# The first eight row tiles of the input projection multiplied before their normalisation is known

## The chip, the cores and the metric

One core of one Trainium2 chip. The time is the device time of one execution in microseconds (us), three executions of the kernel before: 811.78, 812.30 and 813.51 us, median 812.3 us. The profile is of a fourth execution.

## The reference, cut to what matters

One layer: modulated RMSNorm, one input projection, two groups of heads, one output projection, residual, a last RMSNorm. Only the first two matter here, and of the projection only the columns of the convolution group.

```
mod_lat = silu(c) @ w_ada + b_ada             # 2048 x 6144
sh_l, sc_l, gt_l = split(mod_lat, 3)
hl = rmsnorm(x, norm_g) * (1 + sc_l) + sh_l    # x: 512 tokens x 2048
bl, cl, ul, gl, vl, ql = split(hl @ w_in)      # 2048 x 6144
ya = bl * conv(cl * ul) * silu(gl)
```

Everything is float32. With r the reciprocal root of a token's mean square and g = norm_g * (1 + sc), a column of the product is the sum over the 2048 rows k of w[k] * (x[k] * g[k] * r + sh[k]). The factor r belongs to the token and is the same for every k; the shift belongs to k and is the same for every token.

## The kernel before, in words

All activations lie transposed: 128 features on the partitions, 512 tokens along the free axis, so the 2048 rows of the projection are 16 row tiles, k = 0 to 15. A float32 product is taken as three matmuls of rounded parts (`mm3`, lines 81 to 85): weights and activations are split into a high and a low part, and high*high, low*high and high*low are added up in one accumulator (PSUM).

Stage A (lines 343 to 365) runs row tile by row tile over seven column tiles (`A_TILES`), with seven accumulators `acc[0]` to `acc[6]` open over all 16 rows. Before row k can be multiplied, TensorE computes its modulation from 2 MB of `w_ada`: `ada(k)` (line 216) is 64 small float32 matmuls into the accumulator tile `aux`, 128 records in the trace. VectorE turns them round (`ada_t`, line 226: `mods`, `gs`, `sh`); VectorE and ScalarE form the normalised row `x*gs*rinvB + sh` and split it (`h_lat`, line 271: tiles `xhi`, `hlo`). The weights of the row (`raw`, 448 KB) are split by ScalarE and VectorE (`split_a`: `whi`, `wlo`). In each turn k the order on TensorE is: column tile 0 of row k, `ada(k+1)`, column tiles 1 to 6 of row k.

Ahead of stage A stands the statistic: all 16 blocks of x are loaded first (line 98, 256 KB each), squared in turn by VectorE and ScalarE (lines 240 and 242) and summed by TensorE (line 246); four columns of mean squares go through `rsqrt_cols` (line 174) and are spread by TensorE to `rinvB`, 128 x 512 (lines 250 to 262). `ada(0)` and the first row follow.

All loads are issued by SP in program order. The modulation weights `rada` have six buffers of 1 MB (three rows), so the load of row k+3 waits until `ada(k)` has read its own; `raw` has five buffers.

After stage A, stage BC (line 616 on) multiplies the other column tiles piece by piece with the same 16 split rows, which therefore stay in memory; the seven accumulators of stage A are read in its first turns by the functions `ev_c`, `ev_u`, `ev_b`, `ev_g` (lines 388 to 413). Context rows are loaded in turns 12 and 13 of stage A, squared by ScalarE (`ctx_sq`), added by GpSimd (line 295), and summed by TensorE (line 300) in stage BC's turn 2.

Of the kernel before, what the change touches and what calls it, by code (L numbers as in the profile page):

```python
# [16 lines left out]
T = 512  # L17
# [26 lines left out]
N_D = 32  # L44
N_GT = 32
NHC = 3


@with_exitstack
def tile_hybrid_layer(ctx, tc, xt, ct, xn, wada, wgt, bgt, wa_, wbc, wout, lruw, par, ident, fg, out):  # L50
# [10 lines left out]
    hc = s_ctx.enter_context(p_ctx)  # L61
    ctx.enter_context(tc.manual_schedule())
# [31 lines left out]

    xl, xc = [], []
    for k in range(KT):
        t = hl.tile([128, T], F32, name="xhi", bufs=17)
        nc.sync.dma_start(t, xt[k])
        if k == 5:
            nc.sync.dma_start(pt, par)  # L100
            nc.sync.dma_start(idt, ident)
        xl.append(t)
    rawa, rawq = {}, {}
# [84 lines left out]
    gq = [None]  # L188

    def split_a(k):  # L190
        wsp["a", k] = split(rawq.pop(("a", k)), NA * 128)

    def first_operands():

        n, raw, x = NA * 128, rawq.pop(("a", 0)), xl[0]
        whi = stage.tile([128, 1024], F32R, name="whi", bufs=3)
        wlo = stage.tile([128, 1024], F32R, name="wlo", bufs=3)
        hi = hl.tile([128, T], F32R, name="xhi", bufs=17)
        lo = hl.tile([128, T], F32R, name="hlo")
        nc.scalar.copy(whi[:, :n], raw[:, :n])  # L200
        nc.vector.scalar_tensor_tensor(x, x, gs[:, 0, 0:1], rinvB, op0=ALU.mult, op1=ALU.mult)
        nc.scalar.activation(hi, x, AF.Identity, bias=sh[:, 0, 0:1])  # L202
        nc.vector.tensor_tensor(wlo[:, :n], raw[:, :n], whi[:, :n].bitcast(F32), op=ALU.subtract)
        nc.vector.scalar_tensor_tensor(lo, x, sh[:, 0, 0:1], hi.bitcast(F32), op0=ALU.add, op1=ALU.subtract)
        wsp["a", 0], hlat[0] = (whi, wlo), (hi, lo)

    for g in range(3):
        for p in range(2):
            load_ada(g, p)
        load_wa(g)  # L210

# [3 lines left out]

    def ada(g):

        o = aux[:, 64 * (g % 2):64 * (g % 2) + 64]
        for p in range(2):
# [16 lines left out]

    for k in range(KT):
        sq = ta.tile([128, T], F32, name="sq", bufs=3)
        if k % 2:
            nc.vector.tensor_tensor(sq, xl[k], xl[k], op=ALU.mult)  # L240
        else:
            nc.scalar.activation(sq, xl[k], AF.Square)
        if k == 8:
            silu_c()
        j = k % 4
        nc.tensor.matmul(acc[6][32 * j:32 * j + 32, :], ones32, sq, start=k < 4, stop=k >= KT - 4,
                         skip_group_check=True)
    warm(3)
    ssum = ta.tile([128, T], F32, name="sq", bufs=3)
    nc.vector.tensor_copy(ssum, acc[6])  # L250
    for j in range(4):
        nc.tensor.matmul(acc[5][:, 2 * j:2 * j + 2], ssum[:, 128 * j:128 * j + 128], cmean[:, 0:2],
                         start=True, stop=True, skip_group_check=True)
    ms = ta.tile([128, 4], F32, name="ms")
    nc.vector.tensor_scalar(ms, acc[5][:, 0:8:2], EPS, None, op0=ALU.add)
    rl = rsqrt_cols(ta, ms, 4, "l")
    ada(0)
    ada_t(0)
    for j in range(4):
        nc.tensor.transpose(acc[4][:, 128 * j:128 * j + 128], rl[:, j:j + 1].to_broadcast([128, 128]), idt)  # L260
    rinvB = ta.tile([128, T], F32, name="rinvB", bufs=1)
    nc.scalar.copy(rinvB, acc[4])
    warm(8)

    def make_h(k, v, x, rb, n, hi, lo):
        nc.vector.scalar_tensor_tensor(x, x, gs[:, k, v:v + 1], rb, op0=ALU.mult, op1=ALU.mult)  # L266
        nc.scalar.activation(hi, x, AF.Identity, bias=sh[:, k, v:v + 1])  # L267
        nc.vector.scalar_tensor_tensor(lo, x, sh[:, k, v:v + 1], hi.bitcast(F32), op0=ALU.add,
                                       op1=ALU.subtract)

    def h_lat(k):
        hi = hl.tile([128, T], F32R, name="xhi", bufs=17)
        lo = hl.tile([128, T], F32R, name="hlo")
        make_h(k, 0, xl[k], rinvB, T, hi, lo)
        hlat[k] = (hi, lo)
# [138 lines left out]

# [416 lines left out]
```

## Time and profile before

| | |
|---|---|
| median of three runs | 812.3 us |
| profiled execution, its own time | 810.92 us |
| its span | 809.1 us |
| TensorE matmuls busy | 786.8 us (97%), 5712 records |
| VectorE busy | 480.4 us (59%) |
| ScalarE busy | 366.8 us (45%) |
| GpSimd busy | 89.7 us (11%) |

The span is cut into 40 equal slices of 20.2 us in the page; in the first five the 16 DMA engines are busy nine tenths or more of the time, and TensorE is at 7 to 9 tenths. From stage BC on TensorE is at 9 tenths in every slice but the last. The profiled execution's time is 1.8 us more than its span, which begins and ends with the first and last instruction.

### The profile page before, as it was taken

The page shows a single profiled execution, that of the slowest core. Times are in us where ns is not written, and L with a number is a line of the kernel's source. Part 1 is how long each engine was busy: PE and PEld are TensorE (multiplying, and loading weights), DVE is VectorE, ACT ScalarE, POOL GpSimd, SP SyncE. Part 2 cuts the span into 40 slices and gives each one's busy share as a digit, 9 for nine tenths or more (in the row PEclk, how much of TensorE's full clock was granted, in tenths as well). Part 3 has the DMA queues.
Part 4 walks back from the last instruction along what each step waited for, and adds up shares of the span by engine and source line. Part 5 has one row for each costly group of instructions (what it writes and reads, how often), then busy time and mean ns, then how long its engine had stood idle before and what let it go on. Part 6 is the DMA issues. An engine that isn't in the chain of part 4 may idle for free.

```text
span 809.1 us, 13525 instructions
## 1 busy us (share of the span) xinstructions
PE 786.8 (97%) x5712; PEld 678.2 (84%) x5712; DVE 480.4 (59%) x643; ACT 366.8 (45%) x458; POOL 89.7 (11%) x64
## 2 busy tenths in 40 slices
PE   7899899999999999999999999999999999999995
PEld 2688687889999998888888888888888888888884
DVE  3644444888688677283829474666476834253665
ACT  4312224451111125768576857575858532222234
POOL 0000002500000000212020202020212002020200
PEclk9999999999999999999999999999999999999999
DMA  9999996225655664232323232323231753323205
GB/s 352 417 417 415 347 353 218 98 79 187 227 184 180 226 222 153 79 116 80 120 76 122 96 121 79 118 78 118 79 124 58 309 185 92 116 81 128 79 0 208
DMA packets 36494, 136.31 MB, mean 168 GB/s; under 512 B 4049, under 2 KB 6353, under 8 KB 31697
## 3 DMA queue, kind: packets, MB, share of 16 engines
q1 hardware_dynamic: 36434, 135.45, 47.0%
q8 instruction: 45, 0.74, 0.4%
q14 instruction: 15, 0.12, 0.0%
HBM read 131.24 MB, written 4.19 MB: 167 GB/s over the span
## 4 chain that ended last, share of the span: by engine, by line
PE 95%; DMA 1%; DVE 1%; issue 1%; ACT 1%; SPq 0%; ACTq 0%
PE bacc L83 22%; PE bacc L84 22%; PE bacc L85 21%; PE bacc L741 6%; PE bacc L742 6%; PE bacc L743 6%; PE bacc L223 4%; DMA xhi<-in_xt 1%; PE plru L470 1%; PE plru L468 1%; PE plru L85 1%; PE plru L742 1%; PE plru L741 1%; PE plru L84 1%; PE plru L83 1%; PE plru L743 1%
## 5 line engine op out<-in xcount | busy, mean ns | idle before, releaser
L84 PE MATMUL bacc<-xhi,wlo 128*128 128x512 f32 x736 | 280.5, 381 | 2.4 <-issue 1.8
L83 PE MATMUL bacc<-xhi,whi 128*128 128x512 f32 x736 | 281.0, 382 | 0.8 <-ACT xhi L202 0.4
L85 PE MATMUL bacc<-hlo,whi 128*128 128x512 f32 x736 | 279.2, 379 | 2.6 <-issue 2.5
L74 DVE TENSOR_TENSOR wlo<-raw,whi 128x1024 fp32r<-128x1024 f32 (+1 forms) x129 | 157.6, 1225 | 198.9 <-ACT whi L73 197.6
L73 ACT CAST whi<-raw 128x1024 fp32r<-128x1024 f32 (+1 forms) x129 | 132.7, 1031 | 211.6 <-PE bacc L85 116.3
L84 PEld LDWEIGHTS bacc<-xhi,wlo 128*128 128x128 f32 x736 | 139.1, 189 | 25.2 <-DVE wlo L74 5.1
L85 PEld LDWEIGHTS bacc<-hlo,whi 128*128 128x128 f32 x736 | 139.1, 189 | 22.7 <-issue 2.9
L83 PEld LDWEIGHTS bacc<-xhi,whi 128*128 128x128 f32 x736 | 139.1, 189 | 22.5 <-ACT whi L73 0.7
L741 PE MATMUL bacc<-whi,yhi 128*128 128x512 f32 x224 | 85.1, 380 | 0.5 <-DVE dg L671 0.5
L742 PE MATMUL bacc<-wlo,yhi 128*128 128x512 f32 x224 | 84.9, 379 | 0.0
L743 PE MATMUL bacc<-whi,ylo 128*128 128x512 f32 x224 | 84.9, 379 | 0.0
L478 POOL TENSOR_TENSOR li<-li,xb 128x768 f32<-128x768 f32 x16 | 30.8, 1925 | 365.3 <-ACT li L475 365.3
L474 ACT ACTIVATE lr<-plru,pt 64x768 f32<-64x768 f32 x32 | 28.7, 895 | 53.2 <-PE plru L471 53.0
L267 ACT ACTIVATE xhi<-xhi,sh 128x512 fp32r<-128x512 f32 x15 | 10.8, 723 | 85.9 <-DVE xhi L266 85.9
L741 PEld LDWEIGHTS bacc<-whi,yhi 128*128 128x128 f32 x224 | 42.3, 189 | 7.1 <-DVE dg L671 1.1
L743 PEld LDWEIGHTS bacc<-whi,ylo 128*128 128x128 f32 x224 | 42.3, 189 | 6.0
L742 PEld LDWEIGHTS bacc<-wlo,yhi 128*128 128x128 f32 x224 | 42.3, 189 | 6.0
L518 DVE SCALAR_TENSOR_TENSOR gacc<-raw,cs,gacc 128x1024 f32<-128x1024 f32 x32 | 39.6, 1278 | 0.0
L223 PEld LDWEIGHTS bacc<-rada,cs 128*32 128x32 f32 x2048 | 29.6, 110 | 6.8 <-issue 6.8
L84 PE MATMUL bacc<-xchi,wlo 128*128 128x256 f32 x128 | 35.2, 275 | 0.0
L85 PE MATMUL bacc<-hclo,whi 128*128 128x256 f32 x128 | 35.2, 275 | 0.0
L83 PE MATMUL bacc<-xchi,whi 128*128 128x256 f32 x128 | 35.2, 275 | 0.0
(168 smaller groups left out, 876.3 us busy)
## 6 DMA issues: line engine op xcount, KB each, us to landing
raw<-in_wbc SPq DMA_DIRECT2D x82, 512.0 KB, 3.5
rada<-in_wada SPq DMA_DIRECT2D x32, 1024.0 KB, 10.4
raw<-in_wgt SPq DMA_DIRECT2D x32, 512.0 KB, 4.7
raw<-in_wout SPq DMA_DIRECT2D x32, 512.0 KB, 3.5
raw<-in_wa_ SPq DMA_DIRECT2D x16, 448.0 KB, 11.2
xhi<-in_xt SPq DMA_DIRECT2D x16, 256.0 KB, 4.5
xr<-in_xn SPq DMA_DIRECT2D x4, 1024.0 KB, 7.7
xchi<-in_ct SPq DMA_DIRECT2D x16, 128.0 KB, 4.4
```

Source lines behind the costliest of these rows:

```text
L73: nc.scalar.copy(hi[:, :n], raw[:, :n])
L74: nc.vector.tensor_tensor(lo[:, :n], raw[:, :n], hi[:, :n].bitcast(F32), op=ALU.subtract)
L83: nc.tensor.matmul(acc, wh, hh, start=first, stop=False)
L84: nc.tensor.matmul(acc, wl, hh, start=False, stop=False)
L85: nc.tensor.matmul(acc, wh, hl, start=False, stop=last)
L223: nc.tensor.matmul(o[32 * q:32 * q + 32], cs[:, 8 * p + j, :], r[:, j, q, :], start=p + j == 0, stop=p + j == 8, skip_group_check=True)
L474: nc.scalar.activation(lru["r", d][o], pf[0:64, :TA], AF.Sigmoid, bias=b[0:64])
L478: nc.gpsimd.tensor_tensor(lru["i", d], lru["i", d], xb[m], op=ALU.mult)
L518: nc.vector.scalar_tensor_tensor(gacc[:, s], gtq.pop(i), cs[:, k, 0:1], gacc[:, s], op0=ALU.mult, op1=ALU.add)
L741: nc.tensor.matmul(accs[t], yh[:, ts], wh, start=kk == 0, stop=False)
L742: nc.tensor.matmul(accs[t], yh[:, ts], wl, start=False, stop=False)
L743: nc.tensor.matmul(accs[t], yl[:, ts], wh, start=False, stop=kk == KT - 1)
```

## The change

Rows 0 to 7 are multiplied without r and without shift: `h_early` forms and splits `x*gs` alone. When row 7 is done, each of the seven accumulators is multiplied in place by `rinvB` (`scale_acc`). The share of the shift of these rows, the sum over k of sh[k]*w[k], is gathered by VectorE over the raw weights (`z_acc`, tile `zt`, 128 x 896), summed over the partitions by seven matmuls (`z_sum`) into `bz`, and comes in as a bias when the accumulators are read (`ev_c`, `times`). Rows 8 to 15 are made as before. Since stage BC needs all 16 rows normalised, `h_lat(k-8)` makes the early rows again in turns 8 to 15.

The statistic is moved into the rows: x is loaded in groups of three with the rows (`X_ROWS`), squared by ScalarE alone and added by GpSimd (`x_sq`); in turn 6 two matmuls with a matrix of ones (`lat_stat`) give the sum on all partitions, and `lat_rsqrt` takes the root and the reciprocal on 128 x 512 elements. The order of a turn on TensorE becomes: column tiles 0 to 2, `ada(k+1)`, column tiles 3 to 6. `split_a(k+1)` is moved to the start of the turn, ahead of `ada_t(k+1)`.

```diff
+EARLY = 8
+X_ROWS = [0, 3, 3, 3, 3, 3]
...
+    def load_row(r):
+        for _ in range(X_ROWS[r] if r < len(X_ROWS) else 0):
+            load_x()
+        load_ada(r, 0)
+        load_wa(r)
+        load_ada(r, 1)
...
+    def x_sq(k):
+        if k == 0:
+            nc.scalar.activation(sqa, xl[k], AF.Square)
+            return
+        t = te.tile([128, T], F32, name="sq", bufs=3)
+        nc.scalar.activation(t, xl[k], AF.Square)
+        nc.gpsimd.tensor_tensor(sqa, sqa, t, op=ALU.add)
+    def lat_stat(a, b):
...
+        nc.tensor.matmul(aux[:, :b - a], onesr.bitcast(F32), sqa[:, a:b], start=True, stop=True,
+                         skip_group_check=True)
+        nc.vector.tensor_scalar(st["ms"][:, a:b], aux[:, :b - a], 1.0 / D, EPS, op0=ALU.mult, op1=ALU.add)
+    def lat_rsqrt():
...
+        nc.scalar.activation(u, ms, AF.Sqrt)
+        nc.vector.reciprocal(rinvB, u)
+        nc.vector.tensor_tensor(u, rinvB, rinvB, op=ALU.mult)
+        nc.vector.tensor_tensor(u, u, ms, op=ALU.mult)
+        nc.vector.tensor_scalar(u, u, -0.5, 1.5, op0=ALU.mult, op1=ALU.add)
+        nc.vector.tensor_tensor(rinvB, rinvB, u, op=ALU.mult)
+    def scale_acc(j):
+        a = acc[j].rearrange("p (b a) -> p b a", a=2)
+        nc.vector.tensor_tensor(a, a, pairs(rinvB), op=ALU.mult)
+    def z_acc(k):
...
+            nc.vector.scalar_tensor_tensor(zt, raw, sh[:, k, 0:1], zt, op0=ALU.mult, op1=ALU.add)
+    def z_sum():
+        for j in range(NA):
+            nc.tensor.matmul(aux[:, 2 * j:2 * j + 2], zt[:, 128 * j:128 * j + 128], onesr.bitcast(F32)[:, 0:2],
+                             start=True, stop=True, skip_group_check=True)
+        nc.vector.tensor_copy(bz[:, :NA], aux[:, 0:2 * NA:2])
+    def h_early(k):
...
+        nc.scalar.activation(hi, x, AF.Copy, scale=g)
+        nc.vector.scalar_tensor_tensor(lo, x, g, hi.bitcast(F32), op0=ALU.mult, op1=ALU.subtract)
...
+    split_a(0)
+    ada(0, (0,))
+    warm(20)
+    ada(0, (1,))
     ada_t(0)
+    h_row(0)
+    warm(14)
...
     for k in range(KT):
+        if k + 1 < KT:
+            split_a(k + 1)
+        else:
+            split_piece(0)
+        if k == EARLY:
+            z_sum()
+        while n_sq < min(KT, 1 + sum(X_ROWS[:k + 1])):
+            x_sq(n_sq)
+            n_sq += 1
+        if k >= EARLY:
+            h_lat(k - EARLY)
         main_a(k, 0)
+        if k == EARLY - 2:
+            lat_stat(0, 384)
+        main_a(k, 1)
+        main_a(k, 2)
+        if k == EARLY - 2:
+            lat_stat(384, T)
+            lat_rsqrt()
+        if k == EARLY - 1:
+            for j in range(3):
+                scale_acc(j)
         if k + 1 < KT:
             ada(k + 1)
             ada_t(k + 1)
-            h_lat(k + 1)
-            split_a(k + 1)
+            h_row(k + 1)
         if k + 4 < KT:
+            load_row(k + 4)
...
+        for j in range(3, NA):
             main_a(k, j)
+        if k == EARLY - 1:
+            for j in range(3, NA):
+                scale_acc(j)
...
-    evq = [lambda n=n, m=m, j=j: EV[n](m, acc[j]) for j, (n, m) in enumerate(A_TILES)]
+    evq = [lambda n=n, m=m, j=j: EV[n](m, acc[j], bz[:, j:j + 1]) for j, (n, m) in enumerate(A_TILES)]
```

The loads at the head of SP's queue before (`xhi` is x, `pt` and `idt` are constants, `rada` the modulation weights, `raw` the weights of a row):

```order
L98 DMA xhi<-in_xt 128x512 x6
L100 DMA pt<-in_par 128x192
L101 DMA idt<-in_ident 128x128
L98 DMA xhi<-in_xt 128x512 x10
L107 DMA rada<-in_wada 128x2048 x2
L112 DMA raw<-in_wa_ 128x896
```

and now (`xlo` is x):

```order
L108 DMA xlo<-in_xt 128x512
L213 DMA pt<-in_par 128x192
L214 DMA idt<-in_ident 128x128
L115 DMA rada<-in_wada 128x2048
L120 DMA raw<-in_wa_ 128x896
L115 DMA rada<-in_wada 128x2048
L108 DMA xlo<-in_xt 128x512 x3
```

Row 0's weights now stand behind one block of x instead of sixteen, and three blocks stand ahead of each of rows 1 to 5.

VectorE before, one turn of stage A from `ada_t(k+1)` to the split of row k+1's weights:

```order
L228 STREAM_TRANSPOSE mods<-bacc 128x64
L229 TENSOR_SCALAR gs<-mods,bsc_124,pt 128x2
L230 TENSOR_SCALAR sh<-mods,pt 128x2
L266 SCALAR_TENSOR_TENSOR xhi<-xhi,gs,rinvB 128x512
L268 SCALAR_TENSOR_TENSOR hlo<-xhi,sh 128x512
L74 TENSOR_TENSOR wlo<-raw,whi 128x896
```

VectorE now, from the statistic in turn 6 to the low part of row 7 (`sq_983` is the mean square, `bacc_110` is `aux`):

```order
L263 TENSOR_SCALAR sq_983<-bacc_110 128x384
L263 TENSOR_SCALAR sq_983<-bacc_110 128x128
L269 RECIPROCAL rinvB_147<-sq_994 128x512
L270 TENSOR_TENSOR sq_994<-rinvB_147 128x512
L271 TENSOR_TENSOR sq_994<-sq_994,sq_983 128x512
L272 TENSOR_SCALAR sq_994<-sq_994 128x512
L273 TENSOR_TENSOR rinvB_147<-rinvB_147,sq_994 128x512
L235 STREAM_TRANSPOSE mods_1065<-bacc_110 128x64
L236 TENSOR_SCALAR gs_144<-mods_1065,bsc1_104,pt_79 128x2
L237 TENSOR_SCALAR sh_145<-mods_1065,pt_79 128x2
L298 SCALAR_TENSOR_TENSOR elo_1070<-xlo_96,gs_144,xhi_1069 128x512
```

The modulation of row 7 now stands behind the seven instructions of the statistic.

VectorE now, from the scaling in turn 7 to the bias in turn 8 (`mods_1172` is row 8's modulation, `xlo_1179` its low part, `bacc_111` to `bacc_115` and `plru_116` the accumulators):

```order
L277 TENSOR_TENSOR bacc_111<-bacc_111,rinvB_147 128x512
L277 TENSOR_TENSOR bacc_112<-bacc_112,rinvB_147 128x512
L277 TENSOR_TENSOR bacc_113<-bacc_113,rinvB_147 128x512
L235 STREAM_TRANSPOSE mods_1172<-bacc_110 128x64
L236 TENSOR_SCALAR gs_144<-mods_1172,bsc1_104,pt_79 128x2
L237 TENSOR_SCALAR sh_145<-mods_1172,pt_79 128x2
L304 SCALAR_TENSOR_TENSOR xlo_81<-xlo_81,gs_144,rinvB_147 128x512
L307 SCALAR_TENSOR_TENSOR xlo_1179<-xlo_81,sh_145,xhi_1176 128x512
L277 TENSOR_TENSOR bacc_114<-bacc_114,rinvB_147 128x512
L277 TENSOR_TENSOR bacc_115<-bacc_115,rinvB_147 128x512
L277 TENSOR_TENSOR plru_116<-plru_116,rinvB_147 128x512 x2
L291 COPY bz_97<-bacc_110 128x7
```

Three scalings stand ahead of row 8's modulation and four behind its low part; the copy of the bias sums, which frees `aux`, comes after all seven.

## Rows read from the trace of the kernel before

**Rows 1.** Stretches (us): busy time (instructions) of each engine, clock, DMA share, GB/s.

```profile
0.00:10.00 10.00, 5.95 (x14) 1.09 (x14) 3.21 (x8) 3.80 (x5) 0.20 (x4) 1.00 0.83 291
9.00:11.00 2.00, 1.95 (x6) 0.41 (x6) 0.69 (x1) 1.27 (x3) 0.00 (x0) 1.00 1.04 380
10.00:20.00 10.00, 8.04 (x41) 2.84 (x43) 3.91 (x10) 5.17 (x7) 0.00 (x0) 1.00 1.04 414
40.00:60.00 20.00, 19.57 (x443) 16.01 (x442) 9.09 (x18) 3.82 (x5) 0.00 (x0) 1.00 1.02 417
```

**Rows 2.** Timeline of the start: start, length, engine, line, idle time before.

```profile
19.90 1.99 PE L223 MATMUL bacc<-rada,cs 128*32 128x64 f32 x128
24.69 0.48 PE L83 MATMUL bacc<-xhi,whi 128*128 128x512 f32 x1 [0.43 <-ACT xhi L202]
```

**Rows 3.** Chain that ended last, stage A: start, length, what; ada(7) is at 70.74.

```profile
36.34 2.46 issue
...
63.86 1.92 PE bacc L223 x128
...
70.74 1.92 PE bacc L223 x128
...
73.07 0.22 PE bacc L84
...
81.25 1.76 issue
...
88.09 0.84 issue
```

**Rows 4.** Timeline, VectorE and ScalarE in one turn of stage A.

```profile
79.61 0.25 DVE L228 STREAM_TRANSPOSE mods<-bacc 128x64 f32<-128x64 f32 x1 [2.75 <-PE bacc L223]
...
80.22 0.75 DVE L266 SCALAR_TENSOR_TENSOR xhi<-xhi,gs,rinvB 128x512 f32<-128x512 f32 x1
...
81.82 0.75 DVE L268 SCALAR_TENSOR_TENSOR hlo<-xhi,sh 128x512 fp32r<-128x512 f32 x1 [0.85 <-ACT xhi L267]
82.65 1.09 DVE L74 TENSOR_TENSOR wlo<-raw,whi 128x896 fp32r<-128x896 f32 x1
```

**Rows 5.** Groups by shape: count, busy us, mean ns, idle before.

```profile
L179 ACT ACT_TABLE_LOAD x2 | 2.6, 1283 | 0.0
L708 DVE TENSOR_SCALAR xr<-xr,w 128x512 f32<-128x512 f32 x4 | 1.9, 482 | 0.0
L404 DVE TENSOR_TENSOR yA<-yA,bacc 128x512 f32<-128x512 f32 x7 | 4.8, 680 | 0.0
L153 DVE RECIPROCAL w<-w 128x16 f32<-128x16 f32 x1 | 0.3, 253 | 0.0
L180 DVE RECIPROCAL rq_rc<-rq_sc 128x2 f32<-128x2 f32 x1 | 0.2, 166 | 0.3 <-ACT rq_sc L179 0.3
```

**Rows 6.** Timeline of the start: float32 matmuls of two columns, eight records.

```profile
18.92 1.05 PE L252 MATMUL plru<-cmean,sq 128*128 128x2 f32 x8
```

**Rows 7.** Timeline, end of stage A (row 15) and start of stage BC.

```profile
131.22 1.81 POOL L377 MEMSET gacc<- 128x2048 f32 x1 [130.77 <-DMA raw<-in_wbc]
131.48 1.57 DVE L229 TENSOR_SCALAR gs<-mods,bsc,pt 128x2 f32<-128x2 f32 x1
...
136.66 0.48 PE L84 MATMUL bacc<-xhi,wlo 128*128 128x512 f32 x1 [0.64 <-DVE wlo L74]
...
141.08 0.38 PE L83 MATMUL bacc<-xhi,whi 128*128 128x512 f32 x1
```

**Rows 8.** Lines by source: context sums on GpSimd and TensorE, ns, first and last start.

```profile
L295 POOL TENSOR_TENSOR xb<-xb x15: 728/733/1602, 138.1 to 152.9; 128x256 f32<-128x256 f32 x15
...
L300 PE MATMUL bacc<-cmean,xb x4: 168/251/251, 156.6 to 156.9; 128*128 128x2 f32 x4
```

**Rows 9.** Timeline, last matmul; and a stretch behind it (clock last but two).

```profile
800.16 0.38 PE L743 MATMUL bacc<-whi,ylo 128*128 128x512 f32 x1
...
806.00:807.00 1.00, 0.00 (x0) 0.00 (x0) 0.00 (x0) 0.00 (x0) 0.00 (x0) 0.50 1.06 416
```

More of the change, by code (lines that the diff above doesn't have):

```diff
@@ L60, in tile_hybrid_layer @@
     hl = s_lat.enter_context(p_lat)
-    hc = s_ctx.enter_context(p_ctx)
+    te = s_early.enter_context(p_early)
+    hc = []
     ctx.enter_context(tc.manual_schedule())
@@ L93, in pc, with load_x @@
         return pt[:, o + i:o + i + n]
[L95 to L102, printed above, removed]
+    xc = []
+    xl = {k: hl.tile([128, T], F32, name="xlo", bufs=17)
+          for r in range(EARLY) for k in (EARLY + r, r)}
+    n_x = [0]
+    def load_x():
+        nc.sync.dma_start(xl[n_x[0]], xt[n_x[0]])
+        n_x[0] += 1
     rawa, rawq = {}, {}
@@ L188, in tile_hybrid_layer @@
     gq = [None]
+    NAW = NA * 128
+    rawz = {}
     def split_a(k):
[L191 to L210, printed above, removed]
+        raw = rawq.pop(("a", k))
+        wsp["a", k] = split(raw, NAW)
+        if k < EARLY:
+            rawz[k] = raw
+    def load_row(r):
[4 more added lines that the diff above has]
+        load_ada(r, 1)
+    load_x()
+    nc.sync.dma_start(pt, par)
+    nc.sync.dma_start(idt, ident)
+    load_row(0)
+    for r in range(1, 3):
+        load_row(r)
     gs = const.tile([128, KT, 2], F32, name="gs")
@@ L214, in tile_hybrid_layer, with ada @@
     hlat, hctx = [None] * KT, [None] * KT
-    def ada(g):
+    def ada(g, parts=(0, 1)):
         o = aux[:, 64 * (g % 2):64 * (g % 2) + 64]
-        for p in range(2):
+        for p in parts:
             r = rawa.pop((g, p))
@@ L235, in warm @@
             nc.tensor.matmul(acc[0][:, :128], idt, idt, start=True, stop=True)
[L237 to L240, printed above, removed]
-        else:
[L242 to L257, printed above, removed]
-    ada_t(0)
-    for j in range(4):
-        nc.tensor.transpose(acc[4][:, 128 * j:128 * j + 128], rl[:, j:j + 1].to_broadcast([128, 128]), idt)
@@ L261, in tile_hybrid_layer @@
[L261 to L275, printed above, removed]
+    sqa = te.tile([128, T], F32, name="sqa", bufs=1)
@@ new lines, in h_early, with h_lat @@
+    def h_early(k):
+        hi = hl.tile([128, T], F32R, name="xhi")
+        lo = te.tile([128, T], F32R, name="elo")
+        x, g = xl[k], gs[:, k, 0:1]
+        nc.scalar.activation(hi, x, AF.Copy, scale=g)
+        nc.vector.scalar_tensor_tensor(lo, x, g, hi.bitcast(F32), op0=ALU.mult, op1=ALU.subtract)
+        hlat[k] = (hi, lo)
+    def h_lat(k):
+        hi = hlat[k][0] if hlat[k] else hl.tile([128, T], F32R, name="xhi")
+        x, b = xl[k], sh[:, k, 0:1]
+        nc.vector.scalar_tensor_tensor(x, x, gs[:, k, 0:1], rinvB, op0=ALU.mult, op1=ALU.mult)
+        nc.scalar.activation(hi, x, AF.Identity, bias=b)
+        lo = hl.tile([128, T], F32R, name="xlo", bufs=17)
+        nc.vector.scalar_tensor_tensor(lo, x, b, hi.bitcast(F32), op0=ALU.add, op1=ALU.subtract)
+        hlat[k] = (hi, lo)
@@ L386, in rows, with ev_c, times, ev_u @@
         return ap.rearrange("p (r w) -> p r w", w=GRID_W)
-    def ev_c(m, ps):
+    def ev_c(m, ps, b=None):
         cur["c"] = tq[0].tile([128, T], F32, name="ctile")
-        nc.scalar.copy(cur["c"], ps)
-    def ev_u(m, ps):
+        if b is None:
+            nc.scalar.copy(cur["c"], ps)
+        else:
+            nc.scalar.activation(cur["c"], ps, AF.Identity, bias=b)
+    def times(o, a, ps, b):
+        if b is None:
+            nc.vector.tensor_tensor(o, a, ps, op=ALU.mult)
+        else:
+            nc.vector.scalar_tensor_tensor(o, ps, b, a, op0=ALU.add, op1=ALU.mult)
+    def ev_u(m, ps, b=None):
         cu = tq[0].tile([128, T], F32, name="cutile")
-        nc.vector.tensor_tensor(cu, cur["c"], ps, op=ALU.mult)
+        times(cu, cur["c"], ps, b)
         y = yp.tile([128, T], F32, name="yA")
@@ L401, in ev_u, with ev_b, gate, ev_g @@
         nc.vector.scalar_tensor_tensor(yr[:, :, :-1], cr[:, :, 1:], w(2), yr[:, :, :-1], op0=ALU.mult, op1=ALU.add)
-    def ev_b(m, ps):
-        nc.vector.tensor_tensor(yA[m], yA[m], ps, op=ALU.mult)
-    def gate(y, ps):
+    def ev_b(m, ps, b=None):
+        times(yA[m], yA[m], ps, b)
+    def gate(y, ps, b=None):
         sgt = tq[0].tile([128, T], F32, name="sgt", bufs=1)
-        nc.scalar.activation(sgt, ps, AF.Sigmoid)
-        nc.vector.tensor_tensor(sgt, sgt, ps, op=ALU.mult)
+        nc.scalar.activation(sgt, ps, AF.Sigmoid, bias=0.0 if b is None else b)
+        times(sgt, sgt, ps, b)
         nc.vector.tensor_tensor(y, y, sgt, op=ALU.mult)
-    def ev_g(m, ps):
-        gate(yA[m], ps)
+    def ev_g(m, ps, b=None):
+        gate(yA[m], ps, b)
     def ev_q(m, ps):
```

61 lines of the change are left out of this document (36 added, 25 removed).

## The prediction

> **What bounds the kernel now.** I read the stretches first. In stage A the DMA engines are full (share 1.0, 414 to 417 GB/s) and TensorE is nearly full at once: 19.57 of 20 us between 40 and 60 [rows 1]. The timeline of the start shows why it begins late: ada(0) starts at 19.90 and the first product at 24.69 [rows 2], because 4.2 MB of x are loaded, squared and summed first. From there on the chain that ended last runs through TensorE. From one ada to the next is 70.74 - 63.86 = 6.88 us [rows 3]: 1.92 for ada and 21 products at 0.216 (20 of them, with one restart of 0.1, between 136.66 and 141.08 [rows 7]), together 6.46; the other 0.42 are restarts at each change between ada and products and a short wait. Besides, TensorE stands four times on "issue", three of them 2.46, 1.76 and 0.84 [rows 3]. The first product of stage BC starts at 141.08 [rows 7]. What follows is bound by TensorE and is not changed in its work, so the question is when the new stage A reaches that point.
>
> **The supply of the rows.** Row 0 now needs 256 + 96 + 64 KB (x0 and constants) and 2048 + 448 KB of weights, 2.98 MB. The first 10 us moved 2.91 MB [rows 1]: row 0 is there at about 10 us instead of behind all of x. Each of rows 1 to 5 brings three blocks of x with its weights, 3.34 MB, 8.03 us at 416.5 GB/s. With 7.05 MB by 20 us (291 and 414 GB/s [rows 1]), row 5 (19.7 MB) is complete at 50.4, row 6 (2.56 MB more) at 56.5, row 7 at 62.6. TensorE needs 6.46 and some restarts a row, less than 8.03, so until then it waits for loads, whatever the early start gave; the 2.46 us on "issue" and the warm-up matmuls fall in this waiting and cost nothing. Their cover is 1.4 us a row, five times.
>
> At row 6: the second half of ada(6) can run at 56.5 and ends near 57.6; 12 products of row 5 (2.6), column tile 0 of row 6 (0.75), the first sum over the squares (float32, two passes of 384 columns: 0.32 at the products' rate, 0.65 at half of it, which I take), two column tiles (1.3), the second sum (0.25) and its read by VectorE (0.4) bring ada(7) to **64.3**. If x comes at the 380 GB/s of its first stretch [rows 1] it is 64.9 to 65.2; without the waits between, 63.6. Before, ada(7) was at 70.74 [rows 3], and two column tiles less were done: a lead of 6.4 + 1.3 = 7.7 us.
>
> **What the new turns 6 to 8 cost.** VectorE now makes the root on 512 columns, and row 7's modulation stands behind it. From the read of the sum: a table load on ScalarE 1.28 [rows 5], the root and two hand-overs 0.85 (ScalarE's pass between two VectorE instructions [rows 4]), the reciprocal, three products 3 x 0.68, one scalar pass 0.48 [rows 5], modulation to gs 0.47, ScalarE's high part 0.85 [rows 4]. The reciprocal has only small rows: 253 ns for 16 columns, 166 for 2 [rows 5], 6.2 ns a column; 512 columns are 0.166 + 510 x 0.0062 = 3.33 us. The lower end is a pass like any other, 0.69. I take 3.33, since the slope is the instruction's own. Sum: 9.3 us. Beside it TensorE has ada(7) and 12 products, 4.5 us; it waits 4.8, and 0.4 more for the low part: **5.2**.
>
> [...]
>
> From row 7's first product VectorE has: low part 0.85, the shift's share 1.1 (as the split, 1.09), split of row 8's weights 1.09, three scalings of accumulators 2.04 (a product that reads PSUM, 0.68 [rows 5]), modulation 0.61, row 8 in three steps 2.35 [rows 4], four scalings 2.72, split 1.09, bias copy 0.16: 12.0 us. TensorE in this time has 9 products, ada(8), 12 products, the bias sums (14 records at 1.05/8 [rows 6], 1.8) and 9 products, 10.9 with restarts. ada(9) writes where the copy reads and waits 1.1; row 9's low part is 0.4 late: **1.5**.
>
> **Turns 9 to 15.** VectorE's turn grows from 79.61 to 83.74, 4.13 us [rows 4], by the early row made again, 2.35, to 6.5; with hand-over gaps I take 6.8. TensorE's own turn is 6.46 + 0.2 of restarts (I keep half of the 0.42). VectorE is then the slower by some 0.2, seven times 1.4. The work is hidden under TensorE but for that.
>
> **Smaller terms.** GpSimd's clearing of gacc (1.81 us at 131.22) ran beside the modulation of row 15, and one VectorE instruction of it took 1.57 [rows 7], where the whole modulation otherwise takes 0.61 [rows 4]; it is released by the same ada as before, and I charge 1.3 (0 if it meets nothing). The two later stalls on "issue", 2.6 in all, should recur after as many instructions, in turn 7 or 8, where TensorE partly waits for VectorE anyway: 0.9 (0 to 2.6). The 15 squares added by GpSimd lie in rows of 8 us with some 4 us of VectorE work. Bias operands at the reads of the accumulators: 0.06 each, under TensorE. The context squares start later, because row 7 is made again in turn 15; GpSimd's sums were done at 153.6, 3.0 us before TensorE read them at 156.6 [rows 8], and come some 3.5 us later: 0.5 (0 to 0.7).
>
> **The sum.** From ada(7) to the end of stage A: nine ada 17.3, 201 products 43.4, restarts 9 x 0.2, together 62.5; root 5.2, bias sums 1.8, turn 8 1.5, turns 9 to 15 1.4, clearing 1.3, issue 0.9: 74.6. 64.3 + 74.6 = 138.9 against 141.08, with the context 139.4: 1.7 us earlier. The profiled execution took 810.92 (span 809.1 and 1.8 around it) and would take 809.2; the median of the runs shown is 812.3, 1.4 above it, so **810.6 us**. A measurement of this kernel can tell about 0.2% from no change, 1.6 us.
>
> **The rivals.**
> B, the lead is kept: the reciprocal costs a plain pass (2.6 less) and no stall on "issue" is left (0.9 less), 807.1. For it: nothing in the trace shows a long reciprocal on many columns. Against: the slope of 6.2 ns.
> C, VectorE becomes the bound of turns 9 to 15: its 6.8 us need ScalarE twice a turn. If ScalarE's split of the next weights (about 0.9 us) stands in front of one of the two high parts, half of it, 0.5, is added each turn; seven turns give 3.5, 814.1, slower than before. It decides as soon as VectorE's turn exceeds the 6.88 of before. For it: 6.8 is within 0.1 of that. Against: the cast is issued behind the high part and has a gap of its own.
> [...]
> E, the reciprocal is steeper on many columns than the small rows show: each further ns a column is 0.5 us, two of them 811.6. For it: the rows end at 16 columns. Against: they lie on one line. [...]
>
> **Chances.** Forecast as summed (own range 809 to 812.5) 0.32, B 0.29, C 0.21, D 0.09, E 0.09. Faster by over 0.2% (below 810.7): B and 0.15 of the forecast, 0.44. Within: 0.17 of the forecast, 0.06 of D and 0.07 of E, 0.30. Slower (above 813.9): C, 0.03 of D, 0.02 of E, 0.26. The range: down to B and a supply without waits (0.7) and a clearing that meets nothing, 806; up to C with a later x, 815.
>
> **What would show it.** The first product before 20 us; ada(5) and ada(6) waiting for loads, some 8 us apart from each other before row 6; ada(7) near 64; RECIPROCAL near 3.3 us and behind it the longest wait of TensorE in the stage, near 5 us, the clock at full level; turns 9 to 15 6.7 to 6.9 us apart; the first product of stage BC near 139. It would be wrong if the loads were not the limit of rows 1 to 5 (ada(7) before 62), if VectorE's chain ran beside TensorE's work, or if turns 9 to 15 left 6.9.

## The result and the profile after

The changed kernel took 816.63 us in the median of five runs (816.26 to 818.75), the kernel before 811.78 on the same chip (811.58 to 813.51). The ratio is 1.0053, 95% interval 1.0038 to 1.0067: slower by half a percent, where 810.6 us had been forecast. The profiled execution has a span of 814.6 us against 809.1.

Of the 5.5 us between the spans, 4.4 are there when stage BC starts, at 145.45 instead of 141.08, and 1.0 is added after it (the last matmul begins at 805.57, before at 800.16 [rows 7, 9]). Inside stage A the lead falls from place to place: 4.1 us at the first product, 1.3 at ada(7), then minus 4.4.

The start on TensorE, after (timeline: start, length, engine, line, operation, idle time before):

```profile
9.11 1.93 PE L230 MATMUL bacc<-rada,cs 128*32 128x64 f32 x64 [9.11 <-DMA rada<-in_wada]
10.97 5.53 PE L242 MATMUL bacc<-idt 128*128 128x128 f32 x40
16.43 1.10 PE L230 MATMUL bacc<-rada,cs 128*32 128x64 f32 x64
17.46 3.39 PE L242 MATMUL bacc<-idt 128*128 128x128 f32 x28
...
20.61 0.46 PE L89 MATMUL bacc<-xhi,whi 128*128 128x512 f32 x1
```

The two halves of ada(0) stand 7.3 us apart, and the warm-up matmuls (L242) fill the gap: TensorE comes to row 0's first product at 20.61 [rows 2: 24.69]. From there to ada(7) these are all its waits (line, what it waited for, us in total, times, longest; "issue" is time in which the engine waited for nothing that the profile shows):

```profile
PE bacc L230 <- issue: 1.9, 1, 1.9
PE bacc L89 <- ACT xhi L297: 1.8, 1, 1.8
PE bacc L230 <- DVE sq L263: 0.4, 1, 0.4
```

The wait of 1.8 is row 2's first product, held up by softplus (21 small VectorE instructions in turn 0). No wait for a load is among them, though rows 1 to 5 were forecast to be bound by loads. ada(4), ada(5) and ada(6) follow each other by 6.8 and 6.65 us, which is TensorE's own work. Turns 6 to 8 on VectorE, ScalarE and TensorE:

```profile
69.40 1.99 PE L230 MATMUL bacc<-rada,cs 128*32 128x64 f32 x128 [0.38 <-DVE sq L263]
69.43 1.28 ACT L268 ACT_TABLE_LOAD   x1 [3.44 <-DVE sq L263]
...
71.39 3.35 DVE L269 RECIPROCAL rinvB<-sq 128x512 f32<-128x512 f32 x1 [2.04 <-ACT sq L268]
...
78.73 0.80 PE L89 MATMUL bacc<-xhi,whi 128*128 128x512 f32 x1 [4.55 <-ACT xhi L297]
...
92.20 1.99 PE L230 MATMUL bacc<-rada,cs 128*32 128x64 f32 x128 [0.36 <-DVE bz L291]
```

ada(7) is at 69.40 (before 70.74 [rows 3]), the reciprocal takes 3.35 us, and row 7 waits 4.55 us for it. What the wait does besides stands in the stretches (columns as in [rows 1]; the clock is the third number from the end):

```profile
40.00:60.00 20.00, 20.00 (x449) 17.02 (x448) 14.36 (x19) 9.53 (x16) 14.49 (x10) 1.00 1.02 413
74.00:76.00 2.00, 0.18 (x1) 0.00 (x0) 1.86 (x3) 0.00 (x0) 0.00 (x0) 1.00 1.01 413
76.00:78.00 2.00, 0.00 (x0) 0.00 (x0) 1.90 (x6) 0.04 (x1) 0.00 (x0) 0.88 1.00 416
78.00:80.00 2.00, 1.27 (x3) 0.98 (x4) 1.34 (x3) 1.51 (x2) 0.00 (x0) 0.50 1.03 417
...
82.00:84.00 2.00, 2.00 (x47) 1.35 (x49) 1.44 (x3) 0.00 (x0) 0.00 (x0) 0.50 0.45 187
84.00:86.00 2.00, 2.00 (x98) 1.87 (x91) 0.34 (x2) 0.00 (x0) 0.00 (x0) 0.91 0.51 82
```

TensorE is idle from 74.2, and the granted clock is 0.50 from 77.53 to 84.35: row 7's first nine products (78.73 to 82.87) start 0.43 us apart, twice the usual 0.216, and the first part of ada(8) lies in this stretch too (ada(8) takes 2.67 us, ada(7) took 1.99). The end of stage A (timeline):

```profile
137.29 1.57 DVE L236 TENSOR_SCALAR gs<-mods,bsc,pt 128x2 f32<-128x2 f32 x1
...
140.46 0.48 PE L89 MATMUL bacc<-xhi,whi 128*128 128x512 f32 x1 [0.73 <-ACT xhi L305]
...
145.45 0.38 PE L89 MATMUL bacc<-xhi,whi 128*128 128x512 f32 x1
```

Beside the clearing of gacc gs still takes 1.57 us, as in [rows 7], where the gs that starts at 37.03 took 0.29; a wait of 0.73 follows.

### The profile page after: what moved, and what is told of

Its sections match the earlier page's. It is cut to its first block, busy times and chain, and to the rows that moved or that the text cites. A ratio compares the mean times of both kernels' runs of the same rounds, so it can differ in the third digit from the quotient of the medians.

```text
span 814.6 us, 13616 instructions
## 1 busy us (share of the span) xinstructions
PE 783.8 (96%) x5732; PEld 685.4 (84%) x5732; DVE 506.6 (62%) x657; ACT 375.4 (46%) x472; POOL 112.7 (14%) x79
## 4 chain that ended last, share of the span: by engine, by line
PE 90%; DVE 6%; ACT 1%; issue 1%; DMA 1%; SPq 0%; ACTq 0%; DVEq 0%
PE bacc L89 20%; PE bacc L91 20%; PE bacc L90 20%; PE bacc L821 6%; PE bacc L823 6%; PE bacc L822 6%; PE bacc L230 4%; PE bacc L242 1%; DVE wlo L80 1%; PE plru L550 1%; PE plru L548 1%; PE plru L823 1%; PE plru L821 1%; PE plru L822 1%; DMA rada<-in_wada 1%
## 5 line engine op out<-in xcount | busy, mean ns | idle before, releaser
L80 DVE TENSOR_TENSOR wlo<-raw,whi 128x1024 fp32r<-128x1024 f32 (+1 forms) x130 | 161.9, 1247 | 204.3 <-ACT whi L79 203.6
L91 PE MATMUL bacc<-xlo,whi 128*128 128x512 f32 x696 | 264.2, 380 | 0.1
L91 PEld LDWEIGHTS bacc<-xlo,whi 128*128 128x128 f32 x696 | 131.5, 189 | 20.0 <-DVE xlo L307 1.5
L230 PE MATMUL bacc<-rada,cs 128*32 128x64 f32 x2048 | 34.2, 225 | 12.1 <-DMA rada<-in_wada 9.1
L760 POOL TENSOR_TENSOR xr<-xr,fgb 128x512 f32<-128x512 f32 x12 | 18.9, 1596 | 136.9 <-ACT dsq L758 136.9
```

What stands on the lines that cost most here:

```text
L91: nc.tensor.matmul(acc, wh, hl, start=False, stop=last, skip_group_check=skip)
```

## The experiments

All ratios are to the kernel before; the changed kernel's is 1.0053. "Theory T" is at first: TensorE loses time in the early rows to other things than loads, and behind the root to the clock.

### Softplus early

```diff
     silu_c()
+    softplus()
...
-        if k == 0:
-            softplus()
```

> Softplus (21 small VectorE instructions, 7.9 us in turn 0 of the changed kernel) is issued right after silu_c, before row 0's weights are there. Theory T (TensorE loses time in the early rows by things other than loads, and nothing gives it back): the wait of 1.76 us before row 2's first product goes, ada(7) at about 67.6 instead of 69.4, time 814.8 (1.8 less). Rival L (loads bind rows 1 to 5, as the prediction had it): the wait is replaced by a wait for rada, ada(7) stays within 0.4 of 69.4, time 816.6. Rival P (GpSimd's adds are what slows VectorE and other waits take the place of this one): the small instructions run fast in the new place, but wlo stays at 2.17 beside an add; under 1 us gained.

Measured: 1.0029 (1.0018 to 1.004). The wait before row 2 is gone and ada(7) is at 67.72, 1.7 earlier. But part of the lead meets loads, on the second half of ada(5) (timeline):

```profile
53.63 1.10 PE L230 MATMUL bacc<-rada,cs 128*32 128x64 f32 x64 [1.22 <-DMA rada<-in_wada]
```

So softplus's place was worth its wait, as expected, and the load limit is real, only 1 to 2 us behind TensorE.

### Matmuls in the gap

```diff
+            nc.tensor.matmul(acc[3], zero, pairs(hlat[EARLY - 2][0]), start=False, stop=False, skip_group_check=True)
...
+        if k == EARLY - 2:
+            fill(20)
```

> Twenty products with a weight tile of zeros are added to acc[3] at the end of turn 6, so that TensorE has work for 4.3 us while VectorE makes the root; nothing else changes. Theory T: row 7's first product stays at about 78.7, the granted clock stays at 1.00 through 78 to 86, and row 7 and ada(8) end 2.6 us earlier; time 814.0. Rival: the clock's fall costs nothing net, since VectorE's chain of turns 7 and 8 (12 us) is what TensorE waits for there; then the waits at row 8 grow by what the clock gave, and the time stays 816 to 817.

Measured: 1.0018 (1.0006 to 1.0029), 2.8 us less (1.3 to 4.3 by the two intervals). Stretches of this run:

```profile
78.00:80.00 2.00, 2.00 (x11) 1.73 (x10) 1.34 (x4) 1.56 (x2) 0.00 (x0) 1.00 1.04 420
80.00:82.00 2.00, 2.00 (x44) 1.53 (x46) 2.00 (x3) 0.00 (x0) 0.00 (x0) 1.00 0.89 365
```

With useless work in the gap the clock stays at 1.00. ada(9) is at 90.14 instead of 92.20, though ada(7) was 0.2 later: 2.3 us in the profile, although the useless products made row 7 start 0.5 us late (its first product is at 79.46). That is what the fall of the clock cost, apart from the wait itself. Of this, the profiled execution keeps only 0.9 to stage BC (144.59 instead of 145.45): behind a stall of 1.70 on "issue" that ends at 115.08 its products stand 0.43 us apart from 115.7 to 118.7, and the mean of its clock from 100 to 120 is 0.91.

### Root on four columns

```diff
+            nc.tensor.matmul(aux[:, 256 + 2 * j:258 + 2 * j], sqa[:, 128 * j:128 * j + 128], cmean[:, 0:2], ...
+        nc.vector.tensor_scalar(ms, aux[:, 256:264:2], EPS, None, op0=ALU.add)
+        st["r"] = rsqrt_cols(ta, ms, 4, "l")
...
+            nc.tensor.transpose(aux[:, 128 * j:128 * j + 128], st["r"][:, j:j + 1].to_broadcast([128, 128]), idt)
+        nc.scalar.copy(rinvB, aux)
```

> The root is taken on four columns (four small matmuls, rsqrt_cols, four transposes and one copy by ScalarE into rinvB in turn 7) instead of 128 x 512 elements; the statistic's place in turn 6 stays. Theory T: the reciprocal of 3.35 us and the three passes of 0.69 go, the wait of 4.55 before row 7 goes, and with it the fall of the clock (2.6): 7 us less, time 809.5 to 810.5, first product of stage BC near 138.5. Rival (VectorE's chain of turns 7 and 8 binds): the wait comes back behind the scalings, only 4 to 5 us are gained, 812. Rival (only the clock's part is real): 814.

Measured: 1.0003 (0.9988 to 1.0017), 4 us less and not 7. The wait of 4.55 is gone, but TensorE now stands on "issue" (timeline):

```profile
75.33 0.38 PE L91 MATMUL plru<-elo,whi 128*128 128x512 f32 x1 [1.64 <-issue]
...
81.62 0.42 PE L230 MATMUL bacc<-rada,cs 128*32 128x64 f32 x14 [1.74 <-issue]
...
121.15 0.31 PE L230 MATMUL bacc<-rada,cs 128*32 128x64 f32 x6 [2.31 <-issue]
```

With the one at 32.6 these stalls sum to 7.5 us between 10 and 145, against 3.9 in the changed kernel and 5.7 in the kernel before. And the clock falls here too, behind the stall that ended at 81.62 (stretches), as it had behind a wait of 1.50 for softplus that ended at 37.17 (products 0.43 us apart from 38.7 to 40.0, the clock's mean 0.97 from 20 to 40 and 0.95 from 40 to 60):

```profile
82.00:84.00 2.00, 2.00 (x10) 1.70 (x8) 1.33 (x4) 0.50 (x1) 0.00 (x0) 0.77 1.00 412
84.00:86.00 2.00, 2.00 (x6) 1.57 (x5) 1.75 (x3) 1.05 (x2) 0.00 (x0) 0.50 1.01 402
```

This was in none of the three expectations: the gain has the size of the first rival, but not its cause, since no wait for VectorE stands behind the scalings. In the changed kernel, with its wait of 4.55 shortly before, ada(8) has no such stall; why, is said below (Why the prediction was wrong, on "issue").

### No warm-up

```diff
-    warm(20)
...
-    warm(14)
```

> Both groups of warm-up matmuls (20 and 14) are left out. Theory T: ada(0)'s second half starts near 11 instead of 16.4 and the first product near 15 to 17 instead of 20.6; then the rows run 4 to 5 us earlier until the loads stop them, which by the bytes moved is at about 64 for row 7, so 2 to 3.5 us are kept: 813 to 814.5. Rival L (loads bind anyway): the lead is gone at row 3, time 816.6. Rival W (without warm-up the clock stays low through the first rows): first product near 17, products 0.43 apart for several us, time 816 to 819.

Measured: 1.0047 (1.0028 to 1.0065), no change that can be told. The first product is at 15.80 instead of 20.61 and ada(7) at 69.55 instead of 69.40. TensorE's three longest groups of waits from 10 to 70 us:

```profile
PE bacc L89 <- ACT xhi L297: 4.4, 2, 3.0
PE bacc L230 <- DMA rada<-in_wada: 4.0, 3, 1.6
PE bacc L91 <- issue: 1.1, 1, 1.1
```

With the 0.4 for the statistic these are 9.9 us. Of them 1.6 for a load and 1.45 for row 0's high part lie before the first product; 6.8 lie behind it, against 4.1 in the changed kernel. So 2.8 of the 4.8 us went into waits: the wait for softplus grew from 1.8 to 3.0, loads took 2.4, and 0.8 less is on "issue". The other 2.0 went into row 0's products, which stand 0.43 us apart, twice the usual 0.216 (timeline):

```profile
17.25 0.63 PE L89 MATMUL bacc<-xhi,whi 128*128 128x512 f32 x1
17.67 0.63 PE L90 MATMUL bacc<-xhi,wlo 128*128 128x512 f32 x1
```

From 15.80 to ada(1) at 19.94 pass 4.14 us, where the changed kernel takes 2.12 (20.61 to 22.73). That is what rival W forecast for the products, but for one row, and the profile gives the granted clock as 1.00 there; the 2.4 for loads is rival L's. That 2 to 3.5 us would be kept was wrong.

### GpSimd's adds left out

```diff
         nc.scalar.activation(t, xl[k], AF.Square)
-        nc.gpsimd.tensor_tensor(sqa, sqa, t, op=ALU.add)
```

> GpSimd's fifteen adds of the squares are left out (the squares are still made, the sum then holds block 0 alone). Theory T (GpSimd's adds slow VectorE's instructions that run beside them): softplus's three TENSOR_SCALAR of 1.1 to 1.3 us fall to about 0.17, wlo of 2.17 to 1.09, the wait of 1.76 us before row 2's first product goes; ada(7) at about 67.7, ratio to the kernel before 1.003, as with softplus moved. Rival (softplus is long by its own dependent steps, not by GpSimd): its instructions keep their lengths, ada(7) stays at 69.4, ratio 1.005.

Measured: 1.0031 (1.0018 to 1.0043). Softplus on VectorE in the changed kernel, with GpSimd's adds (timeline):

```profile
27.88 0.17 DVE L158 TENSOR_SCALAR w<-w 128x16 f32<-128x16 f32 x1
...
29.19 4.03 POOL L255 TENSOR_TENSOR sqa<-sqa,sq 128x512 f32<-128x512 f32 x3 [28.75 <-ACT sq L254]
29.21 1.31 DVE L165 TENSOR_SCALAR w<-w 128x16 f32<-128x16 f32 x1
...
35.75 1.08 DVE L80 TENSOR_TENSOR wlo<-raw,whi 128x896 fp32r<-128x896 f32 x1
...
39.84 2.17 DVE L80 TENSOR_TENSOR wlo<-raw,whi 128x896 fp32r<-128x896 f32 x1
```

and without the adds:

```profile
28.34 0.17 DVE L158 TENSOR_SCALAR w<-w 128x16 f32<-128x16 f32 x1
...
29.68 0.17 DVE L165 TENSOR_SCALAR w<-w 128x16 f32<-128x16 f32 x1
...
33.19 1.09 DVE L80 TENSOR_TENSOR wlo<-raw,whi 128x896 fp32r<-128x896 f32 x1
...
37.28 1.08 DVE L80 TENSOR_TENSOR wlo<-raw,whi 128x896 fp32r<-128x896 f32 x1
```

Three adds of 1.3 us each meet three scalar passes of 0.17 (1.31, 1.13 and 1.12 beside them), and softplus takes 7.87 us instead of 4.85 (27.88 to 35.75, 28.34 to 33.19); the split of 2.17 ran beside a fourth add. Without the adds TensorE does not wait for softplus, and ada(7) is at 68.39. It is not at 67.7 as expected: ada(1) is 0.5 us later than in the changed kernel (23.19, 22.73), and behind a stall of 1.98 on "issue" that ends at 33.80 products stand 0.43 us apart from 34.9 to 37.9 (the clock's mean from 20 to 40 is 0.91). What each of the three passes loses beside an add (0.95 to 1.14 us) is most of one add (4.03 / 3 = 1.34); by what the two engines hinder each other, no run here shows.

### Softplus early and root on columns together; then without warm-up

The edits are those shown above.

> Softplus behind silu_c and the root on four columns together. If their gains add up (0.0024 and 0.0050 of the time against the changed kernel's 1.0053): ratio 0.998, ada(7) near 67.4, stage BC near 141.5. Rival (stalls on issue in TensorE's stream come back where a wait that covered them goes; they summed to 7.5 us in the run with the root on columns, against 3.9 in the changed kernel): ratio 1.000 to 1.002, with three or four such stalls of 1.6 to 2.3 us.

Measured: 0.9999 (0.9986 to 1.0012), with stalls on issue of 1.80, 1.53, 1.74 and 2.63. ada(7) came at 67.54 and stage BC at 142.03. The sum, 0.998, lies below the interval; the rival's four stalls came, and the lower end of its range, 1.000, lies inside.

> As the run with both, and without the 34 warm-up matmuls. First product near 15. If loads bind rows 4 to 6 (the second half of rada of row 5 landed at 53.6 to 54.0 in two runs, whatever TensorE's lead): ada(6) stays at 59.5, waits for rada grow by what is gained at the start, the same ratio as with both. Theory T in its first form (no load limit): ada(6) at 57 and ratio 0.995.

Measured: 0.9978 (0.9968 to 0.9988), faster than the kernel before. The first product is at 15.53, and now the second half of ada(1) to ada(5) waits for its load, by 0.55 to 1.78 us (timeline; the rows of ada(1), ada(5), ada(6), ada(7) and ada(10)):

```profile
20.95 1.10 PE L230 MATMUL bacc<-rada,cs 128*32 128x64 f32 x64 [0.55 <-DMA rada<-in_wada]
...
53.85 1.10 PE L230 MATMUL bacc<-rada,cs 128*32 128x64 f32 x64 [1.23 <-DMA rada<-in_wada]
...
60.14 2.42 PE L230 MATMUL bacc<-rada,cs 128*32 128x64 f32 x128
...
68.33 1.99 PE L230 MATMUL bacc<-rada,cs 128*32 128x64 f32 x128 [0.25 <-DVE ms L262]
...
96.18 0.30 PE L230 MATMUL bacc<-rada,cs 128*32 128x64 f32 x3 [3.40 <-issue]
```

This is the picture that was forecast for the changed kernel, rows some 8 us apart, but ada(7) is at 68.3 and not at 64.3: row 5 is complete at 53.85 and not at 50.4. The first part of the expectation holds for ada(6), but not for the time, which is 1.7 us (0.0021) below the run with both. The time was not gained by the early start: ada(7) is 0.8 us later than in the run with both (68.33, 67.54), but stage BC is 1.8 earlier (140.25, 142.03). TensorE stands on issue twice in stage A, 3.7 us together (0.26 and 3.40), where the run with both had 7.7. Behind the stall of 3.40 the clock is at 0.50 from 98 to 100.

### x later, and half of x

Both start from the last kernel: softplus early, root on columns, no warm-up. With x later the statistic moves too.

```diff
-X_ROWS = [0, 3, 3, 3, 3, 3]
+X_ROWS = [0, 2, 2, 2, 3, 3, 3]
...
         main_a(k, 1)
         main_a(k, 2)
+        if k == EARLY - 1:
+            lat_spread()
...
         for j in range(3, NA):
             main_a(k, j)
+        if k == EARLY - 2:
+            lat_stat()
```

> As the run with softplus early, root on columns and no warm-up, but x comes in groups 2, 2, 2, 3, 3, 3 with rows 1 to 6 instead of 3 with rows 1 to 5, and the statistic stands at the end of turn 6, its spread behind the third column tile of turn 7. Load theory (rows 1 to 5 wait for loads there): row 5's second half of rada lands 0.79 MB earlier, 1.9 us, near 52; ada(6) near 58.5 instead of 60.1; ratio 0.996. Rival (loads aren't what sets ada(6); TensorE is, with stalls on issue): waits for rada shrink, stalls on issue grow, ratio unchanged at 0.998.

Measured: 0.9963 (0.9951 to 0.9976). Row 5's second half starts at 51.57 (2.3 earlier), ada(6) at 57.85, and the waits of rows 1 to 5 for rada fall from 6.0 us to 3.7 (0.8 more in row 6), while the stalls on issue stay (3.66, 3.73). For the places in the trace the load theory holds; the ratio is 0.0015 lower, which the two intervals, since they overlap, do not show.

```diff
-X_ROWS = [0, 3, 3, 3, 3, 3]
+X_ROWS = [0] + [1] * 15
...
-        while n_sq < min(KT, 1 + sum(X_ROWS[:k + 1])):
+        while n_sq < min(EARLY - 1, 1 + sum(X_ROWS[:k + 1])):
```

> As the run with softplus early, root on columns and no warm-up, with one block of x to a row, so that 1.8 MB of x are not loaded before row 6 is; the statistic then covers seven blocks of sixteen. Load theory: the waits of rows 1 to 5 for rada (6.0 us together in that run) shrink to about 2 or less, row 5 has 10 blocks fewer ahead of it, 2.6 MB or 6.3 us; TensorE can use about 4 of them, ada(7) near 64.5, the place forecast; ratio 0.993 to 0.995. Rival: ada(7) stays near 68, ratio 0.998.

Measured: 0.9961 (0.9947 to 0.9975), ada(7) at 67.61. The waits for rada of rows 1 to 6 are gone; the one that is left is row 0's (the two longest waits from 10 to 70 us):

```profile
PE bacc L91 <- issue: 3.6, 1, 3.6
PE bacc L230 <- DMA rada<-in_wada: 1.6, 1, 1.6
```

A stall of 3.6 on issue stands in row 5 in their place; behind it the clock is at 0.50 from 56 to 58, and behind a second one, of 3.43 up to 95.49, products stand 0.43 us apart from 96.2 to 99.2. So neither expectation came out in full: without the load limit TensorE is stopped on "issue" at nearly the same point (to 53.86, where the wait for row 5's load had ended at 53.85).

### The clearing later

```diff
-    nc.gpsimd.memset(gacc, 0.0)
     for k in range(KT):
         ctx_sq(k)
+    nc.gpsimd.memset(gacc, 0.0)
...
-    at(1, lambda: nc.sync.dma_start(gacc[0:1, :], bgt))
+    at(5, lambda: nc.sync.dma_start(gacc[0:1, :], bgt))
```

> As the run with both, with GpSimd's clearing of gacc put behind its sums of the context's squares (and the load of one row into gacc moved from step 1 to step 5 of stage BC). If the clearing is what lengthens gs and sh of row 15 (1.57 and 1.38 instead of 0.17): they take 0.17, the wait of 0.73 before row 15's first product goes, and stage BC starts 0.7 earlier than in the run with both. Rival (the context's squares' adds take its place, beside the same instructions): no change.

> As the run with softplus early, root on columns and no warm-up, with the clearing of gacc behind the context's sums. The wait of 0.73 before row 15's first product goes; ratio 0.997 (0.0009 less). Rival, by the times of the first pair: no change or 0.001 slower.

> x in groups 2, 2, 2, 3, 3, 3 and the clearing late, both. By the sum of the two expectations 0.995; if neither moves anything 0.998.

Measured: 1.0009 (0.9996 to 1.0021), 0.9989 (0.998 to 0.9997) and 0.9962 (0.9948 to 0.9976); the same kernels without this edit: 0.9999, 0.9978 and 0.9963. The wait of 0.73 before row 15 is gone in all three, but no time shows it. For the third the traces say why: the clearing now runs beside another VectorE instruction, which takes 2.72 us instead of 0.98. With x later, without and then with this edit (timeline; the last row is TensorE's wait for the context's root, 0.45 without it):

```profile
154.15 0.98 DVE L470 TENSOR_SCALAR yA<-cutile,pt 128x512 f32<-128x512 f32 x1
```

```profile
153.14 2.72 DVE L470 TENSOR_SCALAR yA<-cutile,pt 128x512 f32<-128x512 f32 x1
153.78 1.80 POOL L440 MEMSET gacc<- 128x2048 f32 x1
...
161.98 0.40 PE L353 MATMUL bacc<-idt,rq_rc 128*128 128x128 f32 x2 [2.19 <-DVE rq_rc L190]
```

Stage BC starts 1.0 us earlier (138.04, 139.04), and behind this wait TensorE is 0.7 later (161.98, 161.25). The second run shows the same wait, 2.19 instead of 0.46. The profile of the first run doesn't have it (0.45), and why its times don't fall stays open. The kernel with x later is the fastest that leaves nothing out, 810.32 us against 813.05 on its chip; with the clearing late as well it is no different.

## Why the prediction was wrong

**The step that failed** is "until then it waits for loads, whatever the early start gave; the 2.46 us on 'issue' and the warm-up matmuls fall in this waiting and cost nothing", with ada(7) at 64.3. It was at 69.40. (The terms listed for 64.3 add up to 63.55; the other 0.75 stands only in "the waits between". The way from the end of ada(6) to ada(7) came out: 6.7 forecast, 6.7 measured.) Two errors make up the 5.1 us:

- The cover was spent. Warm-up, the late second half of ada(0), 1.9 on issue and 1.8 for softplus kept TensorE behind the loads all the time. Softplus counted: moved, it gave 1.7 at ada(7). The warm-up left out by itself gave nothing there (69.55), so that it cost nothing came true, but by other waits and by row 0's products at half rate. What the 1.9 on issue cost was not tried. That GpSimd's adds would slow VectorE was not in the sum at all: they were put beside "some 4 us of VectorE work" as if the two did not meet.
- The load limit itself lies later, by the other 3.4 (67.72 with softplus moved). The sum counted row 5's 19.7 MB as if they landed in the order of issue. In the run without warm-up the stretch up to the landing says (columns as in [rows 1]):

```profile
0.00:53.85 53.85, 36.18 (x797) 30.01 (x798) 25.79 (x61) 19.12 (x29) 13.53 (x14) 1.00 0.98 386
```

386 GB/s over 53.85 us are 20.8 MB: 1.1 MB of later rows had been moved as well, 2.7 us at 414 GB/s. The rest is the rate: 345 GB/s up to 20 us and 410 up to 40 in that run, where 352 and 416.5 had been taken. Several loads are under way together: up to 70 us in that run the 1 MB loads of rada landed 6.4 to 15.8 us after their issue, 12.2 in the median, where 1 MB at 414 GB/s takes 2.5. That this makes row 5 late was not tried by itself.

**Right in mechanism and size:** the root chain, 9.3 forecast and 9.3 measured (69.43 to 78.73), in it the reciprocal, 3.33 and 3.35; TensorE's wait for it, 4.8 and 4.55. The measured 3.35 decides for the rows' 6.2 ns a column, against B's plain pass and E's steeper slope. Bias sums 1.8 and 1.62. Context 0.5 and 0.44.

**Right in size, not in mechanism:** turns 9 to 15, 6.8 forecast and 6.73 measured. VectorE was to be the slower engine there and to cost 1.4. In the four turns from 92.20 to 119.11 TensorE is busy all the time, VectorE 4.6 to 5.0 us of 6.73, and no wait of its matmuls for VectorE shows; against the 6.65 of the early rows these turns cost 0.08 each. Rival C did not happen.

**The clock fell.** The forecast had it at full level behind the wait, and D, in which it falls there, was given 0.09. Behind the wait of 4.55 it was 0.50 from 77.53 to 84.35; with matmuls in the gap it stayed at 1.00, and the times were 2.8 us less. The trace of before, with its clock at 1.00 from 34 to 42, around the stall of 2.46, could not say so.

**Mis-sized:** turn 8's wait 1.5 against 0.36, the clearing 1.3 against 0.73, stalls on issue behind ada(7) 0.9 against 1.9 (1.58 and 0.35, in turns 12 and 13 and not 7 or 8). From ada(7) to stage BC 76.05 us passed, 74.6 had been forecast. The fall of the clock, which is not in the sum, is more than this 1.5; the terms that were too high take part of it back. That the two ends lie so near is luck.

The balance: of the 7.2 us between the forecast (1.7 earlier) and the profile (5.5 later), 5.1 arose before ada(7), 1.5 from there to stage BC, and 0.6 after it.

**Where the stalls on "issue" stand,** the traces show. Count TensorE's records (weight loads, matmuls and a few semaphore records) from the start: each of the 40 stalls that the timelines of the fourteen runs mark up to 150 us comes after 961 records, or a multiple of 256 more (in the kernel before 961, 1217, 2753, 3009 and 4801, in the changed one 961, 4289 and 4545). And each of the eight in the kernel before and the changed one ends 1.26 to 1.50 us after the end of a transfer of instructions, which the profile lists as a DMA queue of its own (packets, MB, share):

```profile
q8 instruction: 45, 0.74, 0.4%
```

That is 16 KB a packet, and one packet for each 256 of the changed kernel's 11507 TensorE records. So I take these stalls to be waits for TensorE's next instructions; what TensorE stands for at these places the profile does not say. With the root on columns TensorE was at two of the places at 73.7 and 79.9 and stood there 1.64 and 1.74 us. In the changed kernel the transfers of the same turn in the count ended at 74.14 and 80.30, but TensorE, held up by the wait of 4.55, came to the places (after 2497 and 2753 records) only at 80.2 and 85.3, and no stall shows there. So, by this reading, that wait had covered two stalls; their 3.4 us are the size of what the root on columns gained less than the 7 expected. Leaving out the warm-up (68 matmul records and their weight loads) moves all places 136 records on in the work.

**What stays open:** why such a transfer ends when it does. In all fourteen runs the stalls up to 150 us lie before 131, and in five of them (before, changed, root on columns, all three edits, x later) none lies between 145 and 800; up to 142 us the DMA engines are busy seven tenths of the time or more in every slice of the changed kernel's page. That the transfers of instructions compete with the loads would fit this, but no run shows it.

## What to carry to other kernels

When several limits lie within 1 to 2 us of each other (loads, stalls on issue, VectorE's hand-over), removing one buys little: here no edit alone brought the changed kernel below the kernel before, and three together (softplus early, root on columns, no warm-up) did. A term that is called hidden needs the slack it hides in summed against all others that use the same slack. A wait on the critical engine can count twice, once for itself and once for the clock behind it: here 4.55 us, and 2.3 us more in the profile by the clock of 0.50. And before you price its removal, look for what it covers: here, where the wait of 4.55 was gone, two stalls on issue of 1.64 and 1.74 stood.

## What the runs showed of the hardware

- A TensorE wait of 4.55 us, up to 78.73, was followed by a clock of 0.50 up to 84.35. Stalls on issue were followed by a fall too: 1.74 (root on columns, with another of 1.64 six us earlier), 1.98 (adds left out), 3.40 (softplus early, root on columns, no warm-up) and 3.6 (half of x); but not those of 2.46 in the kernel before (1.00 from 34 to 42) and of 1.92 in the changed one (1.00 from 34 to 38).
- The changed kernel's profile lists 45 transfers of instructions, 16 KB each, one for each 256 TensorE records. All 40 stalls on issue up to 150 us in the fourteen runs stood after 961 records or a multiple of 256 more; the eight in the kernel before and the changed one ended 1.26 to 1.50 us after a transfer.
- At the start products stood 0.43 us apart from 16.4 to 19.4 us in the run without warm-up, twice the usual 0.216, while the granted clock was shown as 1.00.
- A GpSimd add of 128 x 512 beside VectorE made a scalar pass of 0.17 us take up to 1.31 and a split of 1.09 take 2.17. A clearing of 128 x 2048 beside it made a scalar pass of 0.98 take 2.72.
